# First half's output projection in seven products, with its differences made beside the second input projection; the second half's takes the convolutions' features first

## The chip, the cores and the metric

The kernel runs on one core of one Trainium2 chip. The metric is the device time of one launch in microseconds (us). A core has a TensorE (PE; its weight loads are PEld), a VectorE (DVE), a ScalarE (ACT), a GpSimd (POOL) and a SyncE (SP), which here does nothing but issue DMAs.

## The reference, cut to what matters

One hybrid decoder block over 2048 positions of width 1024, in float32:

```
h = rmsnorm(x) ; proj = h @ w_in                 # columns q k v g a | c_b c_c c_h
o_gla  = rmsnorm(gated_linear_attention(q, k, v, decay(a))) * silu(g)   # 512 wide, a state runs over the chunks
o_conv = c_b * causal_conv3(c_c * c_h)                                  # 512 wide
x = x + concat([o_gla, o_conv]) @ w_out          # the output projection, 1024 x 1024
h2 = rmsnorm(x) ; x = x + (silu(h2 @ w_gate) * (h2 @ w_up)) @ w_down
out = rmsnorm(x)
```

## The kernel before, in words

Features lie on the partitions. The 2048 positions are four blocks of 512 (b = 0 to 3); blocks 0 and 1 are the first half, 2 and 3 the second. Every float32 operand is split into a high and a low part (`split`, L180 and L193/L194: a ScalarE copy that rounds, then a VectorE subtraction), and each 128x128 by 128x512 product is three matmuls: high by high, high by low, low by high.

The input projection and the feed-forward part run in **units** (`unit`, L464): a 2x2 block of weights (A11, A12, A21, A22) times a 2x2 block of activations (B; its two columns are the two blocks of a half, its two rows the two halves of the feature axis) in seven products instead of eight, by Strassen's method in Winograd's form (`PRODUCTS`). A product is 12 matmuls (L460 to L462), a unit 84. VectorE makes the sums of weights S1 to S4 (L435) and splits them; the activations' differences T1 to T4 are made beforehand. The products' results go through PSUM: c11, c22, c12 are copied out by ScalarE (L500) and completed by VectorE additions (`plus`, L489); with `onto` (as in the down projection) all of it is VectorE additions into tiles that are loaded already. A product that accumulates onto the PSUM tile `oa` or `ob` again must wait until the addition before has read it.

Order of the work: `opening` and `in_proj(0)` (first half, twelve units of 84 less the first two), `in_proj(1)` (twelve units), `out_proj(0)`, `out_proj(1)`, then the feed-forward part. Beside them generators run in the background: `tick`, called after each product or k step, takes a step of `background` at every second call, and at some of the others. The gated attention of a half, `gla_half`, has eight chunks of 128 positions; each has six kinds of small matmul: scores (`sc`), transposes (`kt_ps`, `v_ps`), outputs (`o_ps`), state (`kv`) and a transpose of the result (`ot`). A chunk's inputs are loaded from DRAM scratch with 14 loads of 64 KB (`kq`, `ee`, `vt`, `gt`). `gate(1)` makes the second half's decays (`a_ps`, `z`, scans on VectorE).

`gla_finish` and the end of `in_proj` split the finished features and store both parts in DRAM (`s_gla`, `s_mix`). `out_proj` loads them as pairs (`build_mix`: 16 tiles of 512 KB, names `op<-sgla`, `op<-sm`) and does 8 k steps for each pair of output tiles, without Strassen: 2 x 2 x 8 x 3 = 96 matmuls (L1226, L1227, L1229) for each of four d0, 384 for a half, heads k = 0 to 3 first. VectorE adds the residual (L1251), the result is stored (`s_x1`) and its squares are summed (L1208).

The pool `op` has 28 operand tiles. A unit of `in_proj(1)` uses all 28, so that the next stage's loads wait, tile by tile, for the last unit's products, in the order of `PRODUCTS`. All these DMAs are issued by SP in one order, and each waits for an earlier DMA's semaphore; a load that waits holds up those behind it. The tile framework orders each engine's instructions at build time; on the chip each engine runs its own list in that order.

Of the kernel before, what the change touches and what calls it, by code (L numbers as in the profile page):

```python
# [11 lines left out]
F32 = mybir.dt.float32  # L12
# [8 lines left out]
P = 128  # L21
# [10 lines left out]
LAST_GROUP = GROUPS[-1]  # L32
EARLY = 7
EPS = 1e-6

# [18 lines left out]
def tile_hymba_block(ctx, tc, x, xt, win, wa, wgu, wout, wffn, wdown, wdown_first, small, out):  # L54
# [58 lines left out]
    s_x1 = scratch("sx", KD)  # L113
    s_mix = [[dram.tile([P, 2, PB], F32, name=f"sm{b}_{k}") for k in range(4)] for b in range(NB)]
    s_gla = [dram.tile([P, HEADS, 2, PB], F32, name=f"sgla{b}") for b in range(NB)]
    s_act = [
# [143 lines left out]
    background = []  # L260
    pace, ahead, hurry, steady, hasty = [0], [], [], [], []

# [134 lines left out]
    def weight_quarter(src):  # L397

        n = src.shape[-1]
# [7 lines left out]
        split(src, h[:, 0, :], h[:, 1, :])  # L407
        catch_up()
        return h
# [8 lines left out]
    def unit_weights(src, raw=None, between=()):  # L418
        raw = raw_weights(src) if raw is None else raw
        between = iter(between)  # L420
# [4 lines left out]

        n = src.shape[-1]
        a11, a12, a22, a21 = [raw[:, i, :] for i in range(4)]
        s1 = rawp.tile([P, PB], F32, name="s1", tag="s1", bufs=1)[:, 0:n]
        w = {"A11": weight_quarter(a11)}
# [33 lines left out]

    def unit(src, ops, into=None, onto=None, raw=None, between=(), rest=None):  # L464

# [561 lines left out]
    def in_proj(half, ops, raw=None, between=(), rest=None):  # L1027
# [17 lines left out]
        for i0 in (0, 2):  # L1045
# [134 lines left out]
    def gla_finish(b, t, osb, g):  # L1180
# [12 lines left out]
    def plain_weights(src, n):  # L1193

        raw = rawp.tile([P, 4, PB], F32, name="raw", tag="raw")
        load(raw[:, 0:n, :], src)
        for i in range(n):
# [11 lines left out]

    def build_mix(half):  # L1210
        def pair(b, k):
            return load_pair(s_gla[b][:, k] if k < HEADS else s_mix[b][k - HEADS])

        return [[pair(2 * half + j, k) for j in range(2)] for k in range(KD)]

    def out_proj(half, ops, ahead=None, rest=None):
        ssq = []
        ws = chain.from_iterable(plain_weights(wout[u], 4) for u in range(4))
        for d0 in range(0, KD, 2):
            o = {(e, j): bank() for e in range(2) for j in range(2)}  # L1220
            for k in range(KD):
                for e in range(2):
                    wh, wl = next(ws)
                    for j in range(2):
                        m = ops[k][j]
                        pe.matmul(o[e, j][:], wh, m[:, 0, :], start=k == 0, stop=False)  # L1226
                        pe.matmul(o[e, j][:], wh, m[:, 1, :], start=False, stop=False)  # L1227
                    for j in range(2):
                        pe.matmul(  # L1229
                            o[e, j][:], wl, ops[k][j][:, 0, :], start=False, stop=k == KD - 1  # L1230
                        )
                if k == 3:
# [5 lines left out]
                if half:  # L1238
                    for _ in range(1 if d0 == KD - 2 else 2):
                        next(rest if d0 == KD - 2 else ahead, None)  # L1240
                tick()
# [393 lines left out]
    ssq = out_proj(1, build_mix(1), h2_first(ssq, h2), h2_rest(h2))  # L1635
    ahead.append(h2_ahead(ssq))
# [114 lines left out]
```

## Time and profile before

| | us |
|---|---|
| median of 3 runs (2044.63 to 2045.59) | 2045.29 |
| the profiled execution's own time | 2043.05 |
| its span in the trace | 2041.3 |
| PE busy in the span | 2016.8 |
| PEld busy | 1661.9 |
| DVE busy | 1534.8 |
| ACT busy | 976.4 |

The profiled execution's time is 1.75 us longer than its span. Busy times count an instruction from its start to its modelled end, and pipelined instructions overlap: a matmul of 512 columns shows some 0.39 us, and starts come closer together than that. A row of a window view gives the busy time and number of instructions of each engine in a stretch, the granted TensorE clock, the busy share of the 16 DMA engines, and the GB/s moved. A timeline row gives start, duration, engine, line, output<-inputs, and in brackets idle time ahead of it with its releaser.

### The profile page before, as it was taken

How to read it: one execution, taken by the hardware profiler on the slowest of the kernel's cores; microseconds unless marked ns; L12 is line 12 of the kernel's file. 1: busy time of each engine (PE TensorE's matmuls, PEld its weight loads, DVE VectorE, ACT ScalarE, POOL GpSimd, SP SyncE). 2: the span in 40 equal slices, each digit the busy share in tenths (PEclk: the TensorE clock that was granted, in tenths of full speed). 3: DMA queues.
4: the chain of work that ended last, by engine and by line, in shares of the span. 5: the costliest groups of instructions: out<-in, count | busy, mean ns of one | idle time of the engine just before them, and what ended most of it. 6: DMA issues, size and time to landing. Idle time of an engine off the chain costs nothing.

```text
span 2041.3 us, 26875 instructions
## 1 busy us (share of the span) xinstructions
PE 2016.8 (99%) x9295; PEld 1661.9 (81%) x9295; DVE 1534.8 (75%) x2752; ACT 976.4 (48%) x1936; POOL 11.0 (1%) x17
## 2 busy tenths in 40 slices
PE   9999989999999999999999999999999999999997
PEld 8888878887888888888888888887888888888886
DVE  7888966659744697777777688877777767778886
ACT  6664555756543344444444452334534444454344
POOL 0000000000000000000000000000000000000001
PEclk9999999999999999999999999999999999999999
DMA  7356885524675983546445576576444434486653
GB/s 263 118 202 222 288 302 166 159 81 158 240 250 169 366 303 134 189 152 222 179 146 191 213 281 253 187 280 277 157 168 170 164 141 170 179 331 217 248 217 128
DMA packets 190887, 422.51 MB, mean 207 GB/s; under 512 B 20032, under 2 KB 67360, under 8 KB 181280
## 3 DMA queue, kind: packets, MB, share of 16 engines
q1 hardware_dynamic: 189600, 419.76, 58.1%
q8 instruction: 73, 1.20, 0.2%
q10 hardware_dynamic: 1152, 1.05, 0.2%
q14 instruction: 62, 0.51, 0.1%
HBM read 276.02 MB, written 144.70 MB: 206 GB/s over the span
## 4 chain that ended last, share of the span: by engine, by line
PE 92%; DMA 3%; DVE 3%; ACT 1%; issue 0%; SPq 0%; DVEq 0%; ACTq 0%
PE mm L460 25%; PE mm L462 25%; PE mm L461 25%; PE mm L1226 3%; PE mm L1227 3%; PE mm L1229 3%; PE mm L756 1%; PE a_ps L976 1%; PE mm L757 1%; PE mm L758 1%; PE o_ps L1148 1%; PE o_ps L1150 1%; PE mm L1541 1%; DVE wq L194 0%; PE sc L1124 0%
## 5 line engine op out<-in xcount | busy, mean ns | idle before, releaser
L460 PE MATMUL mm<-op,wq 128*128 128x512 f32 x2443 | 949.3, 392 | 8.7 <-ACT c L500 4.2
L461 PE MATMUL mm<-op,wq 128*128 128x512 f32 x2443 | 949.4, 389 | 0.2 <-DVE op L194 0.2
L462 PE MATMUL mm<-op,wq 128*128 128x512 f32 x2443 | 939.8, 390 | 1.4 <-DVE wq L194 1.2
L193 ACT ACTIVATE wq<-raw 128x512 fp32r<-128x512 f32 (+2 forms) x612 | 357.4, 588 | 602.1 <-PE mm L462 486.7
L460 PEld LDWEIGHTS mm<-op,wq 128*128 128x128 f32 x2443 | 458.5, 188 | 109.6 <-ACT c L500 6.4
L462 PEld LDWEIGHTS mm<-op,wq 128*128 128x128 f32 x2443 | 458.5, 188 | 98.6 <-DVE wq L194 2.7
L461 PEld LDWEIGHTS mm<-op,wq 128*128 128x128 f32 x2443 | 458.7, 188 | 95.2 <-DVE op L194 1.5
L194 DVE TENSOR_TENSOR wq<-raw,wq 128x512 fp32r<-128x512 f32 (+2 forms) x612 | 386.0, 636 | 179.6 <-ACT wq L193 178.2
L489 DVE TENSOR_TENSOR c<-mm,c 128x512 f32<-128x512 f32 x196 | 134.8, 688 | 71.6 <-PE mm L462 64.4
L489 DVE TENSOR_TENSOR y<-mm,y 128x512 f32<-128x512 f32 x185 | 126.7, 688 | 49.7 <-PE mm L462 49.2
L500 ACT ACTIVATE c<-mm 128x512 f32<-128x512 f32 x198 | 115.3, 589 | 20.7 <-PE mm L462 16.7
L435 DVE TENSOR_TENSOR raw<-raw 128x512 f32<-128x512 f32 (+2 forms) x192 | 120.3, 632 | 2.2
L193 ACT ACTIVATE wq<-s 128x512 fp32r<-128x512 f32 (+2 forms) x96 | 56.4, 587 | 103.7 <-PE mm L462 98.0
L1226 PE MATMUL mm<-op,wq 128*128 128x512 f32 x256 | 100.7, 397 | 0.4 <-DMA op<-sgla 0.4
L1227 PE MATMUL mm<-op,wq 128*128 128x512 f32 x256 | 99.9, 390 | 0.0
L435 DVE TENSOR_TENSOR s<-raw 128x512 f32<-128x512 f32 (+2 forms) x96 | 60.8, 633 | 35.6 <-DMA raw<-in_wffn_dram 20.0
L1229 PE MATMUL mm<-op,wq 128*128 128x512 f32 x256 | 82.4, 390 | 0.0
L194 DVE TENSOR_TENSOR op<-op 128x512 fp32r<-128x512 f32 x94 | 62.0, 684 | 3.6 <-ACT op L193 3.5
L194 DVE TENSOR_TENSOR wq<-s,wq 128x512 fp32r<-128x512 f32 (+2 forms) x96 | 60.8, 633 | 3.3 <-ACT wq L193 2.5
L435 DVE TENSOR_TENSOR raw<-s,raw 128x512 f32<-128x512 f32 (+2 forms) x96 | 60.8, 634 | 1.4
L193 ACT ACTIVATE op<-op 128x512 fp32r<-128x512 f32 x94 | 54.6, 620 | 7.2 <-DMA op<-sa_T 3.7
L1226 PEld LDWEIGHTS mm<-op,wq 128*128 128x128 f32 x256 | 48.1, 188 | 11.3 <-issue 1.6
(229 smaller groups left out, 1634.8 us busy)
## 6 DMA issues: line engine op xcount, KB each, us to landing
raw<-in_wffn_dram SPq DMA_DIRECT2D x44, 1024.0 KB, 6.0
sa_B<-so SPq DMA_DIRECT2D x47, 512.0 KB, 3.8
op<-sa_B SPq DMA_DIRECT2D x47, 512.0 KB, 7.1
raw<-in_win_dram SPq DMA_DIRECT2D x22, 1024.0 KB, 5.7
sa_T<-so SPq DMA_DIRECT2D x44, 512.0 KB, 4.4
op<-sa_T SPq DMA_DIRECT2D x44, 512.0 KB, 6.9
raw<-in_wdown_dram SPq DMA_DIRECT2D x24, 768.0 KB, 5.4
sx<-y SPq DMA_DIRECT2D x48, 256.0 KB, 3.7
```

The lines of the kernel that those rows point to most:

```text
L193: last_hi[:] = [act.activation(hi, src, AF.Copy)]
L194: last_lo[:] = [dve.tensor_tensor(lo, src, hi.bitcast(F32), ALU.subtract)]
L435: dve.tensor_tensor(*args)
L460: pe.matmul(o[:], wh, xh, start=first and k == 0, stop=False, skip_group_check=True)
L461: pe.matmul(o[:], wh, xl, start=False, stop=False, skip_group_check=True)
L462: return pe.matmul(o[:], wl, xh, start=False, stop=k == n - 1, skip_group_check=True)
L489: last_plus[:] = [dve.tensor_tensor(t[:], o[:], t[:], ALU.add)]
L500: last_out[:] = [act.activation(t[:], o[:], AF.Copy)]
L756: pe.matmul(acc[:], wq[:, 0, c], p[:, 0, :], start=first, stop=False)
L1226: pe.matmul(o[e, j][:], wh, m[:, 0, :], start=k == 0, stop=False)
L1227: pe.matmul(o[e, j][:], wh, m[:, 1, :], start=False, stop=False)
L1229: pe.matmul(o[e, j][:], wl, ops[k][j][:, 0, :], start=False, stop=k == KD - 1)
```

## The change

The first half's output projection becomes four units of seven products (`out_proj_in_sevens`): B is the first half's features (rows: heads k = 0 to 3 and convolution features k = 4 to 7; columns: blocks 0 and 1), 336 matmuls in place of 384. The rounded pairs of the first half are not stored any more: `in_proj(0)` and `gla_finish` for b < 2 store whole features, without a split. A new generator, `mix_differences`, loads them (16 loads of 256 KB), makes T1 to T4 (16 subtractions, 8 splits of T1 and T2) and stores them (24 stores of 256 KB); `tick` steps it at odd calls, from the end of the first half's attention on (`mixes_begin`, ahead of `gate(1)`). `mix_operands` loads all 28 operand tiles: T1 and T2 as pairs of 512 KB, the 20 others whole (256 KB), to be split on arrival: B11 at once, B21, T3, B22 and T4 at `due`. The residuals are loaded after them, for the next unit midway in a unit. `hastened(gla_half(0), 14)` becomes 22. The second half's `out_proj` stays plain, with `LATE_HEADS`: k = 4 to 7 (convolution) first, then the heads. Its core:

```diff
+LATE_HEADS = 4, 5, 6, 7, 0, 1, 2, 3
...
+        elif mixes:
+            next(mixes[0], None)
         elif hasty and pace[0] % 4 == 3:
...
         c22 = copied("c22", ob, (1, 1))
+        due("B21")
         mul(2, oa)
         c12 = copied("c12", oa, (0, 1))
+        if midway is not None:
+            midway()
...
                 dve.tensor_tensor(y[:], c[:], y[:], ALU.mult)
+                if half == 0:
+                    store(s_mix[j][i0 + r][:], y[:])
+                    continue
...
+        if b < 2:
+            store(s_gla[b][:, :, t * P : (t + 1) * P], osb[:])
+            return
...
+    def mix_differences():
...
+        tiles = fetch()
+        yield
+        for k in range(4):
+            b11, b12, b22, b21 = tiles
+            subtract(b11, b12, b11)
+            subtract(b12, b22, b12)
+            store(s_diff["T3"][k][:], b12[:])
+            yield
+            subtract(b22, b22, b11)
+            halved("T1", k, b11)
+            subtract(b21, b21, b22)
+            store(s_diff["T4"][k][:], b21[:])
+            yield
+            halved("T2", k, b22)
+            tiles = fetch()
+            yield
...
+        for _, n in PRODUCTS:
+            ops[n] = [(load_pair if n in ("T1", "T2") else load_undivided)(p) for p in src[n]]
+            if n == "B11":
+                with behind(last_out):
+                    for o in ops[n]:
+                        split(o[:, 1, :].bitcast(F32), o[:, 0, :], o[:, 1, :])
+            elif n not in ("T1", "T2"):
+                undivided[n] = ops[n]
+        return ops
+
+    def out_proj_in_sevens(ops):
...
+        for d0 in range(0, KD, 2):
+            raw = raw_weights(wout[d0 // 2]).rearrange("p a (b e c) -> p (a b) e c", e=2, c=P)
+            quads = [raw[:, 4 * h : 4 * h + 4, e, :] for e, h in ((0, 0), (0, 1), (1, 1), (1, 0))]
+            more = partial(fetch, d0 + 2) if d0 + 2 < KD else None
+            unit(None, ops, onto=onto[d0], raw=quads, midway=more)
...
+        return {k: [pair(2 + j, k) for j in range(2)] for k in LATE_HEADS}
...
-    background.extend([pause(3), hastened(gla_half(0), 14), gate(1, ops)])
+    background.extend([pause(3), hastened(gla_half(0), 22), mixes_begin(), gate(1, ops)])
     in_proj(1, ops)
     drain_background(lambda: (1, PT - 1) in done)
-    ssq = out_proj(0, build_mix(0))
+    ssq = out_proj_in_sevens(mix_operands())
```

What it moves is decided by the order that comes out on each engine. Three places where the prediction stands on it follow.

SP, around the end of the last unit of `in_proj(1)`, before: the last operand pairs of the first half (`op<-sm`), the next attention chunk's 14 loads (the first is shown), and further on the last convolution stores (`sm2_3` is block 2, feature tile 3) and the first residual `y`.

```order
L148 DMA op_5729<-sm0_3_204 128x1024
L148 DMA op_5731<-sm1_3_208 128x1024
L151 DMA sm2_2_211<-hi_5678 128x512
L148 DMA kq_5653<-sk3_0_125 128x128
...
L151 DMA sm2_3_212<-hi_5696 128x512
L151 DMA sm2_3_212<-c11_5199 128x512
L148 DMA y_5837<-in_xt_dram 128x512
L148 DMA raw_6265<-in_wout_dram 128x2048
```

The same place now: `op_5905`, `op_5907`, `op_5909` are T4's tiles for k = 1 to 3.

```order
L157 DMA gt_5802<-sg3_3_168 128x128
L160 DMA sm3_3_216<-hi_5830 128x512
L160 DMA sm3_3_216<-c22_5171 128x512
L160 DMA sm3_2_215<-hi_5836 128x512
L160 DMA sm3_2_215<-c12_5209 128x512
L160 DMA sm2_3_212<-hi_5842 128x512
L160 DMA sm2_3_212<-c11_5340 128x512
L157 DMA op_5905<-sdT4_1_234 128x512
L157 DMA op_5907<-sdT4_2_235 128x512
L157 DMA op_5909<-sdT4_3_236 128x512
L157 DMA y_5911<-in_xt_dram 128x512
```

The stores and the residual kept their places; three operand loads now stand between them, behind the 14 loads of the chunk.

DVE, first unit of the first half's output projection, now (there is no such unit before): L203 are splits of operands (`op_`) and of attention results (`osb_`), L507 is `plus`, `mm_5949` is the PSUM tile `oa` and `y_5911` the residual of the first output; `ot_6145` is an attention transpose on PE.

```order
L1209 SCALAR_TENSOR_TENSOR osb_6014<-ot_6145,sml_99,gt_5629 128x512
L203 TENSOR_TENSOR op_5905<-op_5905 128x512
L203 TENSOR_TENSOR op_5907<-op_5907 128x512
L507 TENSOR_TENSOR y_5911<-mm_5949,y_5911 128x512
L203 TENSOR_TENSOR osb_5717<-osb_5717,gt_5406 128x512
L203 TENSOR_TENSOR op_5909<-op_5909 128x512
L507 TENSOR_TENSOR y_5913<-mm_5963,y_5913 128x512
```

The first addition out of `oa` stands behind two splits of T4's tiles, and T4 is the last product's operand.

PE, the same unit, now: the end of the fourth product (A12 by B21, PSUM tile `mm_6050`), one chunk's small matmuls, and the start of the third product, which accumulates onto `oa` again.

```order
L480 MATMUL mm_6050<-op_5885,wq_5936 128x512
L1148 MATMUL sc_6063<-kq_5799 128x128
L1148 MATMUL sc_6064<-kq_5799 128x128
...
L1154 MATMUL kt_ps_6071<-ident_87,kq_5799 128x128 x2
L1157 MATMUL v_ps_6074<-ident_87,vt_5801 128x128 x4
L1208 MATMUL ot_6145<-ident_87,osb_6014 128x128 x4
L478 MATMUL mm_5949<-op_5871,wq_5933 128x512
```

Ahead of these rows PE has the products by B11 and T1, the transpose `ot_5817`, and one chunk's `o_ps` and `kv`; before the change PE has plain k steps in this place, which wait for nothing but their operand pairs.

More of the change, by code (lines that the diff above doesn't have):

```diff
@@ L113, in tile_hymba_block @@
     s_x1 = scratch("sx", KD)
-    s_mix = [[dram.tile([P, 2, PB], F32, name=f"sm{b}_{k}") for k in range(4)] for b in range(NB)]
-    s_gla = [dram.tile([P, HEADS, 2, PB], F32, name=f"sgla{b}") for b in range(NB)]
+    parts = [[], [], [2], [2]]
+    s_mix = [
+        [dram.tile([P] + parts[b] + [PB], F32, name=f"sm{b}_{k}") for k in range(4)]
+        for b in range(NB)
+    ]
+    s_gla = [dram.tile([P, HEADS] + parts[b] + [PB], F32, name=f"sgla{b}") for b in range(NB)]
+    s_diff = {
+        n: [dram.tile([P, PB] if n in WHOLE else [P, 2, PB], F32, name=f"sd{n}_{k}") for k in range(4)]
+        for n in ("T1", "T2", "T3", "T4")
+    }
     s_act = [
@@ L462, in product_step, with unit @@
         return pe.matmul(o[:], wl, xh, start=False, stop=k == n - 1, skip_group_check=True)
-    def unit(src, ops, into=None, onto=None, raw=None, between=(), rest=None):
+    def unit(src, ops, into=None, onto=None, raw=None, between=(), rest=None, midway=None):
         w = unit_weights(src, raw, between)
@@ L1196, in plain_weights @@
         load(raw[:, 0:n, :], src)
-        for i in range(n):
+        for i in (n // 2 + i if i < n // 2 else i - n // 2 for i in range(n)):
             h = weight_quarter(raw[:, i, :])
@@ L1208, in sum_squares, with mixed, fetch, halved @@
             dve.tensor_tensor(ssq[:], ssq[:], q[:], ALU.add)
-    def build_mix(half):
+    def mixed(b, k):
+        return s_gla[b][:, k] if k < HEADS else s_mix[b][k - HEADS][:]
+    def mix_differences():
+        order = [kj for k in range(4) for kj in ((k, 0), (k, 1), (k + 4, 1), (k + 4, 0))]
+        def fetch():
+            tiles = []
+            for k, j in [order.pop(0) for _ in order[:4]]:
+                tiles.append(bt("h"))
+                load(tiles[-1][:], mixed(j, k))
+            return tiles
+        def halved(n, k, y):
+            hi = bx[0].tile([P, PB], F32R, name="hi", tag="b")
+            with behind(last_out + last_plus):
+                split(y[:], hi[:], y[:].bitcast(F32R))
+            for e, p in enumerate((hi, y)):
+                store(s_diff[n][k][:, e, :], p[:].bitcast(F32))
+        def subtract(y, a, b):
+            with behind(last_plus):
+                dve.tensor_tensor(y[:], a[:], b[:], ALU.subtract)
+        tiles = fetch()
[14 more added lines that the diff above has]
+            yield
@@ L1237, in out_proj @@
                             load(ys[e, j][:], xt[2 * half + j, :, d0 + e, :])
-                if half:
-                    for _ in range(1 if d0 == KD - 2 else 2):
-                        next(rest if d0 == KD - 2 else ahead, None)
+                for _ in range(1 if d0 == KD - 2 else 2):
+                    next(rest if d0 == KD - 2 else ahead, None)
                 tick()
```

63 lines of the change are left out of this document (48 added, 15 removed).

## The prediction

> **What bounds the kernel now.** I read the page's first and fourth parts, then windows of 100 us, then the waits, then timelines of the two places where the change puts its work.
>
> ```profile
> span 2041.3 us, 26875 instructions
> PE 2016.8 (99%) x9295; PEld 1661.9 (81%) x9295; DVE 1534.8 (75%) x2752; ACT 976.4 (48%) x1936; POOL 11.0 (1%) x17
> PE 92%; DMA 3%; DVE 3%; ACT 1%; issue 0%; SPq 0%; DVEq 0%; ACTq 0%
> ```
>
> TensorE carries 92% of the chain that ended last: a matmul taken away is time won, unless PE then waits for something it did not wait for before. What one matmul is worth must not be taken from its 0.39 us duration, but from a full stretch:
>
> ```profile
> 900.00:1000.00 100.00, 100.00 (x443) 82.81 (x442) 79.07 (x126) 44.59 (x78) 0.00 (x0) 1.00 0.51 182
> ```
>
> 443 matmuls in 100 us, at full granted clock (1.00): 0.2257 us each.
>
> **Term 1, the products.** Four units of 84 = 336 matmuls take the place of 384, all of the same 128x512 form. 48 x 0.2257 = **10.8 us less**. Everything else is a question of what PE waits for.
>
> **Term 2, the start of the first unit.** The trace has a place of the same kind: the change from the first to the second input projection, where all 28 operand tiles are loaded anew.
>
> ```profile
> 266.09 0.50 PE L460 MATMUL mm<-op,wq 128*128 128x512 f32 x1 [0.29 <-DMA op<-siB]
> 273.95 0.49 PE L460 MATMUL mm<-op,wq 128*128 128x512 f32 x1 [2.14 <-ACT op L193]
> 264.00:268.00 4.00, 3.33 (x14) 2.11 (x13) 2.05 (x3) 1.75 (x3) 0.00 (x0) 1.00 1.03 403
> 268.00:272.00 4.00, 3.81 (x17) 2.82 (x15) 0.08 (x1) 0.77 (x2) 0.00 (x0) 1.00 1.04 400
> 272.00:276.00 4.00, 1.82 (x7) 1.28 (x8) 3.28 (x6) 3.56 (x8) 0.00 (x0) 1.00 1.01 401
> ```
>
> In these 12 us the DMA engines are full (shares 1.01 to 1.04), and PE starts 14 + 17 + 7 = 38 matmuls where 53 fit: 15 x 0.2257 = 3.4 us lost. So such a change of operands is not free. The output projection of before starts at 559.21 without a loss, since a plain k step needs two tiles at a time. Now its first unit needs tiles of all seven kinds within one unit. Let T0 be the end of the last input product. PE's work from there to the third product, which must wait for the addition `y_5911`, is worked out from these rows:
>
> ```profile
> 554.67 0.60 PE L1184 MATMUL ot<-ident,osb 128*128 128x128 f32 x4
> 555.02 0.47 PE L1226 MATMUL mm<-op,wq 128*128 128x512 f32 x1
> 559.21 0.39 PE L1226 MATMUL mm<-op,wq 128*128 128x512 f32 x1
> 563.30 0.38 PE L1148 MATMUL o_ps<-vt,scores 128*128 128x128 f32 x2
> 565.76 0.50 PE L1226 MATMUL mm<-op,wq 128*128 128x512 f32 x1
> 575.75 0.71 PE L1124 MATMUL sc<-kq 64*128 64x128 f32 x8
> 577.02 0.47 PE L1227 MATMUL mm<-op,wq 128*128 128x512 f32 x1
> ```
>
> Three products are 36 x 0.2257 = 8.1 us; `ot` is 555.02 - 554.67 = 0.35, twice; `o_ps` with `kv` 565.76 - 563.30 = 2.46; `sc`, `kt_ps` and `v_ps` 577.02 - 575.75 = 1.27. Together T0 + 12.5 us. When is the addition done? By VectorE's order it follows two splits of T4's tiles; by SP's order T4's last three tiles and the residual itself are issued behind an attention chunk's 14 loads and six stores. The same part of SP's list in before, where T0 = 559.21:
>
> ```profile
> 555.11 5.37 SPq L148 DMA_DIRECT2D kq<-sk  x4
> 565.96 1.86 SPq L148 DMA_DIRECT2D gt<-sg  x4
> 568.21 0.32 SPq L151 DMA_DIRECT2D sm<-c  x1
> 574.74 0.67 SPq L148 DMA_DIRECT2D y<-in_xt_dram  x1
> y<-in_xt_dram SPq DMA_DIRECT2D x2, 256.0 KB, 5.5
> DMA to landing us min/median/max: 2.7/3.7/6.9
> ```
>
> - Upper end: the queue is as slow as before. The residual's load was issued at 574.74, T0 + 15.5, and landed 5.5 us later: T0 + 21.0. With the addition (0.6, below) the third product starts at T0 + 21.6: PE loses 9.1 us.
> - Lower end: SP waits for nothing. T4's first tile is free nine matmuls before T0 (-2.0 us); 14 loads, 6 stores and 3 loads at 1.86/4 = 0.46 us are 10.7, a landing 3.7: T0 + 12.4. Then VectorE's list decides: after the last transpose four instructions of 0.60 stand up to and with the addition, 2.4 us.
>
> The bytes agree with a value between. From the first operand load to this residual SP issues 28 tiles of operands (8 x 512 KB + 20 x 256 KB = 9.4 MB) and 4.9 MB of weights, chunk inputs, stores and the residual, 14.3 MB. The first load can start when the first matmuls of the last unit's first product are done: six products (16.3), some 4.1 of small matmuls and 2.0 ahead of T0, T0 - 22.4.
>
> ```profile
> 552.00:560.00 8.00, 8.00 (x39) 6.61 (x38) 6.70 (x11) 4.08 (x8) 0.00 (x0) 1.00 1.03 422
> 560.00:568.00 8.00, 8.00 (x50) 6.73 (x49) 3.63 (x9) 3.90 (x15) 0.00 (x0) 1.00 0.68 234
> 588.00:596.00 8.00, 8.00 (x44) 6.40 (x43) 5.36 (x16) 4.75 (x16) 0.00 (x0) 1.00 0.95 303
> ```
>
> At 422 GB/s 14.3 MB take 33.9 us (T0 + 11.5), at 303 47.2 us (T0 + 24.8). I take **6.5 us more**, nearer to the upper end, since SP's list is that of before with 9.4 MB of operands for 8.4. After it nothing else is late there: the next units' residuals and weights are issued a unit ahead. [...]
>
> **Term 3, VectorE and the differences.** They are made beside the second input projection.
>
> ```profile
> 461.60 0.68 DVE L194 TENSOR_TENSOR wq<-raw,wq 128x512 fp32r<-128x512 f32 x1
> 462.20 0.69 DVE L435 TENSOR_TENSOR raw<-raw 128x512 f32<-128x512 f32 x1
> 440.00:460.00 20.00, 20.00 (x89) 16.33 (x88) 8.87 (x15) 8.80 (x17) 0.00 (x0) 1.00 0.15 54
> 460.00:480.00 20.00, 19.55 (x87) 15.79 (x86) 20.00 (x41) 18.41 (x41) 0.00 (x0) 1.00 0.28 84
> 480.00:500.00 20.00, 19.23 (x97) 15.43 (x96) 19.00 (x38) 9.04 (x21) 0.00 (x0) 1.00 0.69 224
> 500.00:520.00 20.00, 20.00 (x102) 16.00 (x101) 11.03 (x25) 9.46 (x26) 0.00 (x0) 1.00 0.30 95
> ```
>
> Starts are 0.60 us apart, so 16 subtractions and 8 splits are 14.4 us. VectorE has 80 - 58.9 = 21.1 us free in 440 to 520, but only 1.0 in 460 to 500, where the gates' scans stand and PE already loses 0.45 + 0.77. The change brings the gates forward (22 hastened steps), so part of the free 11 us ahead is used. Bounds: nothing, if all fits the free time; 4.8 us, if the eight or so instructions that fall among the scans push everything back by 0.60 each. I take **1.0 us more**, near the lower end, since PE's additions have a product (2.7 us) of slack. In the four units themselves VectorE gets, beside the attention, 28 weight splits, 20 sums, 28 additions, 14 sums of squares and 16 splits: 106 x 0.60 = 64 us in over 90 us of PE time. That hides, beyond term 2.
>
> **Term 4, ScalarE's tables.** The order of now has 20 table loads, before 15: the hastened attention runs through the silu units.
>
> ```profile
> 411.42 1.28 ACT L200 ACT_TABLE_LOAD   x1
> 412.71 0.20 ACT L200 ACTIVATE hy<-hl 128x4 f32<-128x4 f32 x1
> 410.00:415.00 5.00, 5.00 (x26) 4.18 (x25) 2.77 (x9) 4.93 (x8) 0.00 (x0) 1.00 0.00 0
> ```
>
> Five more at 1.29 us are 6.5 us where ScalarE has little free; PE lost nothing there. Between 0 and 6.5 I take **0.5 more**, nearest to what PE lost. [...]
>
> **Term 5, what goes.** The first half's features are stored once: one 256 KB store fewer lies among the operand loads of 264 to 272 (`sm0_2<-hi`), 0.65 us at 400 GB/s off the loss there, **0.7 less**. The second half now starts on convolution features, which are stored long before; the wait for a head's pair goes:
>
> ```profile
> 666.79 0.47 PE L1226 MATMUL mm<-op,wq 128*128 128x512 f32 x1 [0.35 <-DMA op<-sgla]
> ```
>
> **0.4 less.** The splits of the first half's features and the plain projection's loads were off the chain: nothing.
>
> **Sum.** -10.8 + 6.5 + 1.0 + 0.5 - 0.7 - 0.4 = -3.9 us. From the profiled execution's 2043.05 (span 2041.3 and 1.75 around it) that is 2039.2; the median of the runs, 2045.29, lies 2.24 above that execution, so I predict 2041.4 us.
>
> **The rivals.**
> - A, the start is covered: SP's queue runs ahead as in the lower end, the stall is 2.4, terms 3 and 4 are nothing: -10.8 + 2.4 - 1.1 = -9.5, 2035.8. For it: PE lost only 3.4 us at the like place with 11.5 MB (16 pairs, 12 whole tiles). Against: T4's position.
> - B, two engines fill up: terms 3 and 4 are 4.8 and 1.0 instead of 1.0 and 0.5. -10.8 + 6.5 + 5.8 - 1.1 = +0.4, 2045.7. For it: VectorE's 39.0 of 40 us in 460 to 500. Against: free time on both sides.
> - C, slower: the start of the first unit becomes a DMA stall of its own. If the 14.3 MB move at 270 GB/s, between the 234 and the 303 above, they need 53.0 us, the residual is there at T0 + 30.6, the third product starts at T0 + 31.2, PE loses 18.7: -10.8 + 18.7 + 1.5 - 1.1 = +8.3, 2053.6. It turns slower than before once the residual lands after some T0 + 22. Against: shares near 1.0 come with 400 GB/s in the operand loads.
> - The change does what it says: the order shows 48 matmuls fewer on PE, so I give no chance to that it doesn't.
>
> **How the numbers follow.** My forecast (between -7 and -1.5 us) has 0.43, A 0.25, B 0.18, C 0.14. A measurement of this kernel can tell about 0.2%, 4.1 us, from no change. Faster by more: A and half of the forecast, 0.46. Within: the other half and B, 0.40. Slower: C, 0.14. The range goes from A with the shortest stall, 2035, to the nearer part of C, 2049, with some 0.06 left below and 0.09 above; the forecast's own is 2038.3 to 2043.8.
>
> **What would show it.** PE has 48 matmuls fewer. In the first unit of `out_proj_in_sevens` its third product waits for VectorE's addition into `y`, and that for the load of `y` or a split of `op`: 2.4 to 9 us in one gap. The stretch with the differences has VectorE near full and PE losing 2 to 3 us there; the silu units lose under 1. At 264 to 276 PE loses less than 3.4. I would be wrong if the gap in the first unit were missing, or several units had one, or PE waited for T1's or T2's pairs.

## The result, and the profile after

The changed kernel takes 2061.28 us (median of 5 runs, 2060.57 to 2063.14), the kernel before 2045.29 (5 runs, 2042.75 to 2046.78): a ratio of 1.0085, 95% interval 1.0073 to 1.0096. It is 16 us slower. The profiled execution took 2062.3 us, 19.2 us more in its span than that of before.

The page of the changed kernel: span, busy times, the granted clock in 40 slices of 51.5 us, the chain that ended last.

```profile
span 2060.5 us, 26992 instructions
PE 2014.2 (98%) x9247; PEld 1658.9 (81%) x9247; DVE 1576.0 (76%) x2820; ACT 995.9 (48%) x1965; POOL 11.0 (1%) x17
PE   9999999999879999999999999999999999999997
PEclk9999999999989999999999999999999999999999
PE 72%; DMA 4%; DVE 3%; SPq 0%; issue 0%; ACT 0%; DVEq 0%; ACTq 0%
```

The 48 matmuls are gone (9247 for 9295). Yet TensorE is busy only 2.6 us less, and its share of the chain fell from 92 to 72%: it waits. The eleventh and twelfth slice (515 to 618 us) show an 8 and a 7, and the twelfth a lower clock. TensorE's waits between 390 and 650 us, of after, then all of those of before:

```profile
engine line waited for: us in total, times, longest us
PE sc L1148 <- DVE kq L1138: 13.9, 3, 8.2
PE mm L478 <- DVE y L507: 6.1, 1, 6.1
PE ot L1208 <- DVE osb L1201: 4.9, 2, 3.5
PE mm L480 <- DVE wq L203: 1.5, 1, 1.5
PE mm L478 <- ACT ee L1158: 0.8, 1, 0.8
```

```profile
PE mm L460 <- ACT c L500: 1.2, 2, 0.8
```

From here on **loss** means: the distances between the starts of TensorE's instructions in the timeline, less 0.2265 us for each one of 512 columns and 0.112 for each of 128. (Both are rounded means, so a stretch can come out a few tenths off.)

| loss of TensorE, us | 200-390 | 390-430 | 430-550 | 550-650 | 650-780 |
|---|---|---|---|---|---|
| before | 7.1 | -0.1 | 3.1 | -0.3 | 1.7 |
| after | 3.3 | 6.8 | 15.2 | 14.5 | 1.1 |

29.4 us more were lost and 10.8 saved: 18.6 of the 19.2; the rest is scattered before and after. Three places hold it.

**The silu units (398 to 406).** TensorE and ScalarE, after:

```profile
398.11 0.39 PE L480 MATMUL mm<-op,wq 128*128 128x512 f32 x1
402.03 1.09 PE L1208 MATMUL ot<-ident,osb 128*128 128x128 f32 x4 [3.53 <-DVE osb L1201]
403.34 0.63 PE L479 MATMUL mm<-op,wq 128*128 128x512 f32 x1
403.77 0.63 PE L480 MATMUL mm<-op,wq 128*128 128x512 f32 x1
405.69 0.40 PE L479 MATMUL mm<-op,wq 128*128 128x512 f32 x1
405.93 0.40 PE L480 MATMUL mm<-op,wq 128*128 128x512 f32 x1
```

```profile
397.26 1.28 ACT L208 ACT_TABLE_LOAD   x1
398.56 0.20 ACT L208 ACTIVATE hl<-hsq 128x4 f32<-128x4 f32 x1
399.07 1.28 ACT L209 ACT_TABLE_LOAD   x1
400.36 0.21 ACT L209 ACTIVATE hy<-hl 128x4 f32<-128x4 f32 x1
```

Two table loads stand in the chain from a chunk's outputs over the reciprocal root to `osb`, which the transposes `ot` need. At the faster pace `ot` comes one product earlier on TensorE's list (24 matmuls of 512 columns behind the `kv` ahead of it, where before has 36 and 48 in these units), and finds it unfinished. Both are needed: at 336 us of after, where no table is loaded, `ot` stands behind 24 too and waits for nothing. Behind the wait of 3.53 us the matmuls start 0.43 us apart for some 2.5 us (403.34, 403.77), then 0.24 again; the granted clock is 0.57 from 402 to 406 us. So this wait costs over 1 us more than itself. After the waits of 8.2 and 6.1 us it is the same; together 18 distances of 0.43 stand behind these three, 18 x 0.20 = 3.6 us.

**The differences (490 to 533).** The chain of waits, SyncE's queue and VectorE, after:

```profile
509.90 8.08 DMA sdT<-h
518.00 0.32 SPq L157
522.63 1.92 DMA gt<-sg
525.27 0.34 DVE kq L1138
525.66 1.22 PE sc L1148 x8
```

```profile
512.51 0.85 SPq L160 DMA_DIRECT2D sgla<-gt  x1
517.36 0.33 SPq L157 DMA_DIRECT2D h<-sm  x1
518.00 1.74 SPq L157 DMA_DIRECT2D kq<-sk  x4
```

```profile
510.19 0.68 DVE L203 TENSOR_TENSOR wq<-s,wq 128x512 fp32r<-128x512 f32 x1
516.78 0.69 DVE L453 TENSOR_TENSOR s<-raw 128x512 f32<-128x512 f32 x1 [5.90 <-DMA raw<-in_win_dram]
```

A difference's store takes 8.08 us to land. SyncE's list stands still from 513.4 to 517.4 at the last load of features (`h<-sm`), and the chunk's 14 loads come behind it, the first only when that store has landed. The weights (`raw`), issued at 508.68, land at 516.7; VectorE, which could have caught up, has nothing to do for 5.9 us. Then everything that it was to do comes at once, and the scores wait 8.22 us for `kq`.

**The first unit (577 to 604).** TensorE and VectorE, after:

```profile
588.41 0.39 PE L480 MATMUL mm<-op,wq 128*128 128x512 f32 x1
594.00 1.22 PE L1148 MATMUL sc<-kq 64*128 64x128 f32 x8 [5.21 <-DVE kq L1138]
596.49 1.06 PE L1208 MATMUL ot<-ident,osb 128*128 128x128 f32 x4
603.61 0.80 PE L478 MATMUL mm<-op,wq 128*128 128x512 f32 x1 [6.06 <-DVE y L507]
```

```profile
600.80 1.30 DVE L203 TENSOR_TENSOR op<-op 128x512 fp32r<-128x512 f32 x2 [2.46 <-ACT op L202]
602.86 0.69 DVE L507 TENSOR_TENSOR y<-mm,y 128x512 f32<-128x512 f32 x1 [0.76 <-DMA y<-in_xt_dram]
```

```profile
575.00:590.00 15.00, 13.80 (x75) 10.98 (x73) 15.00 (x28) 11.92 (x29) 0.00 (x0) 1.00 0.87 312
```

T0 is 577.2; the third product starts at 603.61, T0 + 26.4, where 12.5 us of work stand before it. The residual landed at T0 + 25.7 behind two splits of T4, as the order had it; but the chunk's scores wait in the same unit, and VectorE (in the window row, the third number with a count) is busy 15.0 of 15 us.

### The profile page after: what moved, and what is told of

It reads as the page before. It is cut to its first block, busy times and chain, and to the rows that moved or that the text cites. A ratio compares the mean times of both kernels' runs of the same rounds, so it can differ in the third digit from the quotient of the medians.

```text
span 2060.5 us, 26992 instructions
## 1 busy us (share of the span) xinstructions
PE 2014.2 (98%) x9247; PEld 1658.9 (81%) x9247; DVE 1576.0 (76%) x2820; ACT 995.9 (48%) x1965; POOL 11.0 (1%) x17
## 4 chain that ended last, share of the span: by engine, by line
PE 72%; DMA 4%; DVE 3%; SPq 0%; issue 0%; ACT 0%; DVEq 0%; ACTq 0%
PE mm L480 22%; PE mm L478 22%; PE mm L479 22%; PE mm L1343 1%; PE mm L1341 1%; PE mm L1340 1%; DMA op<-sdT 1%; PE mm L1654 1%; DMA raw<-in_wffn_dram 1%; DVE wq L203 0%; SPq L157 0%; DMA op<-shT 0%; DMA sdT<-h 0%; DMA sx<-y 0%; PE a_ps L997 0%
## 5 line engine op out<-in xcount | busy, mean ns | idle before, releaser
L478 PE MATMUL mm<-op,wq 128*128 128x512 f32 x2555 | 997.1, 393 | 12.0 <-DVE y L507 7.1
L479 PE MATMUL mm<-op,wq 128*128 128x512 f32 x2555 | 995.0, 390 | 0.5 <-DVE op L203 0.5
L480 PE MATMUL mm<-op,wq 128*128 128x512 f32 x2555 | 985.1, 390 | 2.2 <-DVE wq L203 1.8
L202 ACT ACTIVATE wq<-raw 128x512 fp32r<-128x512 f32 (+2 forms) x620 | 362.4, 588 | 595.0 <-PE mm L480 508.6
L478 PEld LDWEIGHTS mm<-op,wq 128*128 128x128 f32 x2555 | 480.8, 188 | 117.9 <-DVE y L507 7.9
L480 PEld LDWEIGHTS mm<-op,wq 128*128 128x128 f32 x2555 | 480.7, 188 | 105.1 <-DVE wq L203 4.4
L479 PEld LDWEIGHTS mm<-op,wq 128*128 128x128 f32 x2555 | 481.0, 188 | 100.5 <-DVE op L203 2.8
L203 DVE TENSOR_TENSOR wq<-raw,wq 128x512 fp32r<-128x512 f32 (+2 forms) x620 | 392.9, 638 | 148.5 <-ACT wq L202 146.9
L507 DVE TENSOR_TENSOR y<-mm,y 128x512 f32<-128x512 f32 x213 | 146.2, 689 | 66.0 <-PE mm L480 64.8
L507 DVE TENSOR_TENSOR c<-mm,c 128x512 f32<-128x512 f32 x196 | 135.1, 689 | 62.7 <-PE mm L480 59.9
L453 DVE TENSOR_TENSOR raw<-raw 128x512 f32<-128x512 f32 (+2 forms) x200 | 126.2, 637 | 2.3
L453 DVE TENSOR_TENSOR s<-raw 128x512 f32<-128x512 f32 (+2 forms) x100 | 63.7, 637 | 51.5 <-DMA raw<-in_wffn_dram 28.1
L203 DVE TENSOR_TENSOR op<-op 128x512 fp32r<-128x512 f32 x114 | 75.8, 688 | 7.2 <-ACT op L202 6.8
L202 ACT ACTIVATE op<-op 128x512 fp32r<-128x512 f32 x114 | 66.5, 620 | 12.4 <-DMA op<-sa_T 4.6
L203 DVE TENSOR_TENSOR wq<-s,wq 128x512 fp32r<-128x512 f32 (+2 forms) x100 | 63.7, 637 | 1.8 <-ACT wq L202 1.0
L573 ACT ACTIVATE sg<-mm 128x512 f32<-128x512 f32 x26 | 15.5, 598 | 83.2 <-PE mm L480 83.2
L573 ACT ACTIVATE c<-c 128x512 f32<-128x512 f32 x78 | 49.0, 629 | 11.6 <-DVE c L507 8.6
L1340 PE MATMUL mm<-op,wq 128*128 128x512 f32 x128 | 50.2, 392 | 0.0
L1341 PE MATMUL mm<-op,wq 128*128 128x512 f32 x128 | 49.8, 389 | 0.0
```

What stands on the lines that cost most here:

```text
L202: last_hi[:] = [act.activation(hi, src, AF.Copy)]
L203: last_lo[:] = [dve.tensor_tensor(lo, src, hi.bitcast(F32), ALU.subtract)]
L453: dve.tensor_tensor(*args)
L478: pe.matmul(o[:], wh, xh, start=first and k == 0, stop=False, skip_group_check=True)
L479: pe.matmul(o[:], wh, xl, start=False, stop=False, skip_group_check=True)
L480: return pe.matmul(o[:], wl, xh, start=False, stop=k == n - 1, skip_group_check=True)
```

## The experiments

All are edits of the changed kernel, except where it is said. The losses of their profiled executions by stretch, beside the median and the ratio to the kernel before with its interval (the kernel before was run anew beside each group, at 2043.4 to 2045.3 us, so runs are best compared by the ratio):

| | us | ratio, interval | 390-430 | 430-550 | 550-650 |
|---|---|---|---|---|---|
| after | 2061.28 | 1.0085 (1.0073, 1.0096) | 6.8 | 15.2 | 14.5 |
| e1 | 2058.07 | 1.0072 (1.0057, 1.0087) | 7.1 | 12.1 | 13.3 |
| e2 | 2066.60 | 1.0113 (1.0097, 1.0128) | 6.7 | 15.5 | 17.4 |
| e3 | 2062.04 | 1.0086 (1.0070, 1.0103) | 0.1 | 16.5 | 20.3 |
| e4 | 2044.27 | 1.0001 (0.9991, 1.0010) | 0.1 | 3.0 | 0.7 |
| e5 | 2051.32 | 1.0032 (1.0019, 1.0045) | 7.1 | 2.6 | 16.7 |
| e6 | 2048.28 | 1.0017 (1.0007, 1.0026) | 8.0 | 2.0 | 12.0 |
| e7 | 2049.14 | 1.0025 (1.0015, 1.0034) | 6.9 | 4.5 | 11.2 |
| e8 | 2058.78 | 1.0068 (1.0053, 1.0083) | 7.2 | 4.1 | 21.6 |
| e9 | 2058.36 | 1.0070 (1.0055, 1.0085) | 7.2 | 10.4 | 11.4 |
| e10 | 2060.42 | 1.0077 (1.0060, 1.0094) | 7.1 | 14.0 | 10.9 |
| e11 | 2061.33 | 1.0083 (1.0068, 1.0098) | 0.0 | 14.3 | 14.5 |
| e12 | 2061.34 | 1.0081 (1.0064, 1.0099) | 7.0 | 15.2 | 11.9 |
| e13 | 2062.96 | 1.0089 (1.0074, 1.0104) | 5.5 | 15.9 | 14.6 |
| e14 | 2052.53 | 1.0041 (1.0026, 1.0056) | 8.0 | 14.2 | 5.0 |
| e15 | 2066.43 | 1.0108 (1.0093, 1.0123) | 6.7 | 15.9 | 17.4 |
| e16 | 2066.64 | 1.0110 (1.0093, 1.0127) | 6.4 | 20.9 | 8.2 |
| e17 | 2050.04 | 1.0027 (1.0016, 1.0039) | 6.5 | 6.1 | 12.5 |
| e18 | 2051.02 | 1.0040 (1.0027, 1.0052) | 0.0 | 9.3 | 14.8 |

**e4, the second half alone** (on the kernel before: the new order of k and of the weights).

```diff
-        return [[pair(2 * half + j, k) for j in range(2)] for k in range(KD)]
+        return {k: [pair(2 * half + j, k) for j in range(2)] for k in (LATE_HEADS if half else range(KD))}
```

> The kernel before with only the second half's new order of k (convolution features first). Theory: it takes the wait for a head's pair away and nothing else: PE's loss at 650 to 680 falls from 1.8 to under 0.5 us, the time is 2043.5 to 2045. Rival: the order of k is itself part of the slowdown, since the weights are split in another order: over 2047.

2044.27, no difference. The slowdown is the first half's alone.

**e3, the pace.**

```diff
-hastened(gla_half(0), 22)
+hastened(gla_half(0), 14)
```

> Only the 22 hastened steps go back to 14. Theory T: the loss of 6.8 us at 390 to 425, where the attention's table loads now stand among the silu units and the transposes wait for VectorE (3.5 and 1.4 us), goes to nothing, as before the change. The differences then start later: if there is room, the time is some 2054; if they then meet the gates and the convolutions more tightly, part of it comes back at 480 to 560 and the time is 2055 to 2060. Rival: the loss there has nothing to do with the pace; the time stays within 2059 to 2063.

The loss at 390 to 430 goes as expected, so the table loads and the pace made it: with 14 steps there are 15 table loads again, and `ot` stands behind 36 and 48 matmuls. The time stays: the differences start later, and 1.3 + 5.8 us more are lost further on. Taking a loss away in one stage did not bring time, since the next stage got its work later.

**e5, e6, e7, the differences taken apart.** e5 leaves the generator out; e6 leaves out `subtract` and `split`; e7 leaves out `load` and `store`:

```diff
-background.extend([pause(3), hastened(gla_half(0), 22), mixes_begin(), gate(1, ops)])
+background.extend([pause(3), hastened(gla_half(0), 22), gate(1, ops)])      # e5
-                dve.tensor_tensor(y[:], a[:], b[:], ALU.subtract)                # e6
-                load(tiles[-1][:], mixed(j, k))                                  # e7
-            store(s_diff["T3"][k][:], b12[:])                                    # e7, and the like
```

> The differences T1 to T4 are left out (no loads, no arithmetic, no stores; the products read whole features in their place, so the output is not the block's). All else of the change stays. If the differences make the whole loss at 480 to 560, that stretch falls from 14.4 us to the 1.9 of before, and the time from 2061 to some 2048.5; the loss at 390 to 425 (6.8) and that at 576 to 615 (14.8) stay, since neither has a difference in it. Rival: the loss at 480 to 560 is the attention's, which runs elsewhere now; then over 6 us of it stay and the time is over 2052.

> The differences' 16 loads and 24 stores stay, with their buffers and their places on SP; the 16 subtractions and 8 splits are left out (the stored tiles are the unchanged features, so the output is not the block's). Theory P (transfers and buffers: SP's list, the 11 buffers that they share with the attention's chunk, 10.5 MB more): over half of the 12.4 us that the differences cost at 480 to 560 stays, time 2055 or more. Theory V (VectorE and ScalarE: 14.4 us more work where VectorE had 1.0 free of 40): under a third stays, time under 2053.

> The 16 subtractions and 8 splits stay, on a constant and without any transfer; their 16 loads and 24 stores are left out, and the products read whole features (the output is not the block's). Theory P: under a third of the 12.4 us stays, time under 2053. Theory V: over half stays, time 2055 or more. If the two parts cost about 6 each, or neither costs much alone, it is their chain (a store that waits for VectorE, a chunk's load that waits for the store).

Without the differences 2.6 us are lost at 430 to 550 (before: 3.1), so they make the whole loss there, 12.6 us. Either part alone costs almost nothing: 2.0 us are lost with the transfers, 4.5 with the arithmetic (e7's trace is of its fastest execution, 2.3 us under its median). So it is the two together that cost. How they do is read from the trace above: they are tied to each other, a store waits for VectorE, the next load for the store's landing and for its buffer, the attention's loads and the weights for SyncE's list, and VectorE for the weights. A rival is not excluded by these three runs: that both use up the same spare time, and only their sum exceeds it.

**e1, the differences' transfers on GpSimd's queue.**

```diff
-                load(tiles[-1][:], mixed(j, k))
+                pool.dma_start(tiles[-1][:], mixed(j, k))
-            store(s_diff["T3"][k][:], b12[:])
+            pool.dma_start(s_diff["T3"][k][:], b12[:])
```

> Only the 16 loads and 24 stores of the differences move from SP to GpSimd's own queue; the work on VectorE and ScalarE stays. Theory Q (one queue in order): PE's loss of 12.7 us at 480 to 528 (2.0 before the change) comes from SP's list, in which a difference's load or store waits at the head for VectorE and holds up the weights and the attention chunk behind it; it should fall to 2 to 4 us, and the time from 2061 to some 2051. Rival V (VectorE is full): 16 subtractions and 8 splits push everything back there, whoever issues the transfers; the loss stays over 10 us and the time within 2058 to 2062.

At 430 to 550 12.1 us are lost for 15.2, not 2 to 4; the times can hardly be told apart. Being in one list with the differences is not all of it. In e1 one of SyncE's loads waits 3.3 us for TensorE's `kv`, which releases a chunk's buffer (the differences' tiles share these 11), `ee` lands late again, and ScalarE waits for it. A wait of SyncE, a row of ScalarE and the first of TensorE's waits, all of e1:

```profile
SPq L157 <- PE kv L1179: 3.3, 1, 3.3
```

```profile
494.97 0.42 ACT L1135 ACTIVATE ee<-ee 128x256 f32<-128x256 f32 x1 [2.95 <-DMA ee<-sd]
```

```profile
PE mm L478 <- ACT c L518: 7.2, 3, 5.3
```

Behind `ee` on ScalarE stands the copy of a product's result, and behind that TensorE, 5.3 us.

**e8, T1 and T2 whole.**

```diff
-                split(y[:], hi[:], y[:].bitcast(F32R))
-            for e, p in enumerate((hi, y)):
-                store(s_diff[n][k][:, e, :], p[:].bitcast(F32))
+            store(s_diff[n][k][:], y[:])
-            if n == "B11":
+            if n in ("B11", "T1", "T2"):
```

> T1 and T2 are stored and loaded whole (256 KB) and split on arrival, as the other kinds: 8 splits, 8 buffers and 8 stores fewer beside the second input projection, 2.1 MB fewer among the 14.3 MB at the first unit, and 8 splits of 0.60 us more there, ahead of the second and third product. Theory B (bytes bound the first unit, 2.1 MB at 380 GB/s are 5.5 us): the loss at 576 to 615 falls from 14.8 to 9 or 10, and that at 480 to 560 by 3 to 6, time some 2052. Rival V at that place: the 4.8 us of splits more hold VectorE, which is full at 580 to 596, and the loss at 576 to 615 stays or grows to 19, time 2057 to 2063.

At 430 to 550 the loss falls to 4.1, with 8 splits, 8 buffers and 8 stores fewer, as the tie and its rival would both have it. But the first unit loses 21.6, 19.0 of them in one wait of the attention's transposes for `osb`, which VectorE had behind the splits that were moved there. The rival at that place held.

**e2 and e9, other queues for the operands and for the chunk.**

```diff
+        queues.append(nc.gpsimd)                                   # e2, around the 28 operand loads
-                load(dst[:, i, :], r[:, s])
+                (nc.sync if b < 2 else pool).dma_start(dst[:, i, :], r[:, s])   # e9
```

> Only the 28 operand loads of the first half's output projection move from SP to GpSimd's queue. Theory Q: PE's loss of 14.8 us at 576 to 615 comes from SP's list, where the attention chunk's 14 loads and the residual stand behind operand loads that wait for their tiles; the wait of the scores (5.2 us) goes, the wait for the residual's addition (6.1 us) falls to under 3, and the time falls by 7 to 10 us to some 2053. Rival B (bytes): 14.3 MB have to come in whoever issues them; the loss stays at 12 to 15 us and the time within 2058 to 2062.

> Only the second half's attention chunks' loads (14 of 64 KB each) move from SP to GpSimd's queue. Theory Q (what costs is that a chunk's loads stand in SP's list behind stores of differences, at 480 to 560, and behind operand loads, at 576 to 615): the scores' waits for the scaled kq (13.9 us in all) fall to under 4 us, the time falls by 7 to 11 us to some 2052. Rival (the chunk is only the last of several late things: bytes and VectorE's own list hold the rest): the waits change their names, the time stays over 2057.

With the operands on their own queue the wait for `y` falls to 0.3 us, as expected, but 7.2 us are lost for `osb` instead: VectorE waits 5.8 us for weights that come in beside the operands (its row in e2 below). With the chunk's loads moved, the scores' waits for `kq` are gone, and the wait for `y` grows from 6.1 to 8.0. Moving one transfer ahead put another one last: 11 to 17 us stay.

```profile
580.05 0.69 DVE L455 TENSOR_TENSOR s<-raw 128x512 f32<-128x512 f32 x1 [5.76 <-DMA raw<-in_wout_dram]
```

**e10 and e11, the residual asked for first, and with 14.**

```diff
         onto = {}
         fetch(0)
+        ops = mix_operands()
```

> As the run before, and the first unit's residuals are asked for ahead of the operand loads; VectorE's first addition then stands ahead of the splits of T4. Theory Q: the third product's wait (6.1 us) falls to under 3 as well, and the time to some 2048. Rival B (the 14.3 MB bound the first unit): the loss at 560 to 615 stays over 11 us and the time is within 1 us of the run before.

> As the run before, with 14 hastened steps for 22. The loss of 6.8 us at 390 to 425 goes. With the chunk's loads off SP the later start of the differences costs less than the 6.8 us that it gave back when 14 was tried alone: some 2043 to 2046, as the kernel before or a little under it. Rival: gates, convolutions and differences still meet on VectorE, the gain is given back, within 2 us of the run before.

Nothing gained, but the order that was to be tried did not come out. In the list that SyncE ran in e10 the residual's load still stands behind all 28 operand loads (issued at 586.89, the last operands' from 584.18 to 585.86), and VectorE's first addition behind all 16 operand splits, both as in e9; in e11 it is the same. So these two runs say nothing on a residual that comes first. In e10 VectorE was busy up to the moment at which the residual landed; both were late alike:

```profile
593.29 0.69 DVE L203 TENSOR_TENSOR op<-op 128x512 fp32r<-128x512 f32 x1
594.38 0.69 DVE L507 TENSOR_TENSOR y<-mm,y 128x512 f32<-128x512 f32 x1 [0.40 <-DMA y<-in_xt_dram]
```

**e12, fewer bytes.**

```diff
+            if n == "T2":
+                ops[n] = ops["T1"]
+                continue
```

> T2's four pairs are not loaded, the products read T1's tiles in their place (the output is not the block's): 2.1 MB of 14.3 fewer at the first unit, no instruction of VectorE or ScalarE more or less. Theory B: the loss at 560 to 615 falls by 2.1 MB at some 390 GB/s, 5.4 us, from 14.7 to some 9, time 2056. Theory Q and V (order and VectorE): it falls by under 2 us, time over 2059.

2.6 us less are lost at 550 to 650, half of what the bytes would give; the time does not move. Bytes are a part at most.

**e14, the first unit copied by ScalarE.**

```diff
-            unit(None, ops, onto=onto[d0], raw=quads, midway=more)
+            if d0 == 0:
+                c = {at: bt("c") for at in onto[d0]}
+                unit(None, ops, into=c, raw=quads, midway=more)
+                for at, y in onto[d0].items():
+                    dve.tensor_tensor(y[:], c[at][:], y[:], ALU.add)
```

> Only the first of the four units is changed: its products are copied out of PSUM by ScalarE into fresh tiles and the residuals added afterwards, as many VectorE instructions as before, 4 ScalarE copies more. Theory L (VectorE's list and the residual's load hold the first addition): the wait for the addition into y (6.1 us) goes and nothing as large takes its place; the loss at 576 to 615 falls from 14.8 to 6 to 9, of which the wait for the chunk's kq (5.2) stays; time 2053 to 2056. Rival B (the operands are not there yet): the third product waits for T2's tiles or the fourth for B21's, and the loss stays over 12 us.

This run takes most of the loss at the third place away. Same bytes, same queue, same number of VectorE instructions: the loss falls from 14.5 to 5.0, the time by 8.8 us. The windows of after (above) and of e14:

```profile
575.00:590.00 15.00, 13.94 (x76) 11.09 (x74) 12.72 (x27) 9.38 (x26) 0.00 (x0) 1.00 0.91 334
590.00:605.00 15.00, 14.12 (x63) 11.24 (x64) 14.63 (x26) 12.18 (x25) 0.00 (x0) 0.89 0.98 336
```

TensorE is busy 14.1 us from 590 to 605, where after has 4.9. The wait of 6.1 us was for the instruction that frees the PSUM tile `oa`: with `onto` it is an addition that needs the residual and VectorE's turn, with a copy it needs neither. The wait for the chunk's `kq` (5.2 us), which was to stay, went too, and not through the copy: the lists came out in another order. In e14 the scores stand 48 matmuls of 512 columns behind the `kv` ahead of them, in after 12, and VectorE begins the 16 operand splits at 590.64, in after at 580.23. So the order on the engines, and not the bytes, made most of the loss there; how much of the 8.8 us is the copy's and how much the other order's, this run doesn't tell.

**e13 and e15, arithmetic on GpSimd.**

```diff
+    def split_aside(src, hi, lo):
+        act.activation(hi, src, AF.Copy)
+        return pool.tensor_tensor(lo, src, hi.bitcast(F32), ALU.subtract)
-                dve.tensor_tensor(y[:], a[:], b[:], ALU.subtract)
+                pool.tensor_tensor(y[:], a[:], b[:], ALU.subtract)   # e13; e15: split_aside in `due`
```

> The differences' 16 subtractions and the subtracting half of the 8 splits run on GpSimd (1.30 us each for 128x512 by the page's last part of the kernel, 31 us in all, where it had nothing to do); transfers, buffers and SP's list stay. Theory V with the chain: VectorE is relieved of 24 x 0.60 = 14.4 us, the loss at 425 to 560 (14.9) falls to 3 to 6, time 2050 to 2053. Rival: GpSimd's slower tiles hold their buffers and the queue longer, the attention chunk's loads come later still; the loss stays over 10 us, time over 2057.

> Only the subtracting half of the 16 operand splits in the first unit (B21, T3, B22, T4) runs on GpSimd, 1.30 us each, in place of 0.60 on VectorE. Theory L: VectorE has 9.6 us less to do between 577 and 603, the kq scaling and the first addition come earlier; the loss at 576 to 615 falls to 8 or 10 us, or, if GpSimd's 20.8 us for the 16 become what the fourth product waits for, a new wait of PE for GpSimd's op tiles of 3 to 6 us shows. Rival B: nothing falls, 14 us or more.

No gain in e13, 5 us lost in e15, and neither theory had the reason. A row of each engine in e13, and one of each in e15, at the same time:

```profile
481.26 6.95 POOL L1263 TENSOR_TENSOR h<-h 128x512 f32<-128x512 f32 x4
485.30 1.77 DVE L1091 TENSOR_TENSOR c<-c,c 128x512 f32<-128x512 f32 x1
```

```profile
578.95 3.26 POOL L208 TENSOR_TENSOR op<-op 128x512 fp32r<-128x512 f32 x2 [577.14 <-ACT op L207]
579.28 1.78 DVE L203 TENSOR_TENSOR wq<-raw,wq 128x512 fp32r<-128x512 f32 x1
```

While GpSimd computed, these two instructions of VectorE took 1.77 and 1.78 us, where the same forms take 0.69 in the mean in after (0.71 at most), and GpSimd's own took 1.44 and 1.63 us in the mean in e13, where it takes 1.29 for 128x512 in after. What VectorE was relieved of it lost again: over the whole span it is busy 1576.0 us in after, 1576.8 in e13 with 24 instructions fewer, and 1576.3 in e15 with 16 fewer.

**e16, e17, e18, joined.** e16 is e14 with e9 and e13; e17 is e14 with e8; e18 is e17 with 14 hastened steps.

> e14, the second half's chunk loads on GpSimd's queue (e9) and the differences' subtractions on GpSimd (e13) together. If the three losses are separate: 6.8 at 390 to 425 stays, 480 to 560 falls to 3, 560 to 615 to 3 to 5; time 2043 to 2046, level with the kernel before. Rival: GpSimd's arithmetic holds up the chunk's loads in its one list, and the attention waits again: time over 2050.

> e14 and e8 together: the first unit copied by ScalarE, T1 and T2 whole and split on arrival. If the losses add up: 390 to 425 keeps its 7 to 8 us, 425 to 560 has the 4.2 of e8 in place of e14's 14.3, and the first unit, with 8 splits of 0.60 us more ahead of the second and third product, 4.1 to 9: from e14's 2052.5 to 2043 to 2047. Rival: the 8 splits bring the first unit's wait back whole (e8 had 21.4 us from 560 to 615): over 2055.

> e17 with 14 hastened steps for 22. If the losses add up, the 7 to 8 us at 390 to 425 go, and the differences, which start later, give back 2 to 4 of them: 3 to 6 us under e17, some 2040 to 2042, a little under the kernel before. Rival: as in e3, the differences then run into the convolutions and the first unit, and all of it is given back: within 2 us of e17.

e16 went the rival's way, over 2050: 20.9 us are lost at 430 to 550. e17 is the fastest of all that keep the change and compute the block, 2050.04, still 0.27% slower than the kernel before (0.16 to 0.39%). It lies between its two cases: 6.1 us at 430 to 550, but 9.4 us in one wait for `osb` ahead of the first unit. In e18 that wait stays, the 6.5 us at 390 to 430 go, and 3.2 + 2.3 come back in the next two stretches. The largest waits between 425 and 650, of e17 and of e18:

```profile
PE ot L1208 <- DVE osb L1201: 9.4, 1, 9.4
```

```profile
PE ot L1208 <- DVE osb L1201: 10.0, 1, 10.0
```

The losses do not add up, and no version beats the kernel before.

## Why the prediction was wrong

- **Term 1 held**: 48 matmuls fewer, 10.8 us.
- **Term 5 was small by its size**: -0.7 and -0.4 were given; the loss fell by 3.8 at 200 to 390 (1.9 of it at 264 to 276) and by 0.6 at 650 to 780. In e4, with the second half's order alone, it fell by the same 0.6.
- **Term 2 failed, and it is the largest miss: +6.5 (2.4 to 9.1) against +14.8.** The addition, its place behind T4's splits and the residual's late load were all seen. Two steps failed. First, "After it nothing else is late there": the chunk's 14 loads, which the text itself placed ahead of the residual in SyncE's list, were late themselves, and the scores lost 5.2 us before the addition lost 6.1. Second, "106 x 0.60 = 64 us in over 90 us of PE time. That hides": it was a mean over four units, and a large part of it falls before the first addition; from 575 to 590 VectorE is busy 15.0 of 15. The time that TensorE lost behind such waits in after, 0.20 us for each of 5 to 7 slow matmuls, was in no term. e14, with copies and another order of the lists, loses 9.5 us less there.
- **Term 3 failed: +1.0 (0 to 4.8) against +12.1.** Only the 24 instructions on VectorE were priced. The 40 transfers of the differences were listed with the change and stood in no term, although each waits in SyncE's one list and holds one of 11 buffers. e6 and e7 show that the arithmetic alone, which was priced, costs 1.4 us over before. The two together cost the rest.
- **Term 4 failed, just past its upper bound: +0.5 (0 to 6.5) against +6.9.** "PE lost nothing there" was read at the old pace, where the transposes came a product later. e3 shows the loss goes with the pace.
- **The rivals.** C, the slower one (0.14), came nearest: it had the residual later than T0 + 22, 18.7 us lost, 2053.6. The residual came at T0 + 25.7. But bytes were its reason, and e12 and e14 show them to be a part at most. B gave the second place 4.8 us of its 12.1 and laid it to VectorE's work, which alone costs 1.4 (e7).
- **The signs named in advance**: one gap in the first unit was forecast, there were two; the stretch with the differences was to lose 2 to 3 us and lost 15.2; the silu units were to lose under 1 and lost 6.8. All three say where it was wrong. At 264 to 276 less than 3.4 was to be lost, and 2.3 were.

What stays open: how the 8 us of the store at 509.90 divide between its wait among other transfers and its own time (the DMA engines are busy 0.99 of it, at 303 GB/s); whether the differences cost by the tie or by the sum of their work; how e14's gain divides between the copy and the order; and whether more buffers or a residual that comes first would help, which no run tries.

## What to carry to other kernels

A transfer that waits for arithmetic and an arithmetic instruction that waits for a transfer, in lists that run in order, must be priced together: here each alone cost 0 to 1.4 us and both 12. A share of busy time over a stage does not hide work that is due at its start; count what stands in the list ahead of the instruction that frees the next tile, and let that instruction need as little as possible (a copy for an addition, with the other order of the lists that came with it, was worth 8.8 us). Where a wait is taken away, look what stands next in its engine's list: in most of these runs it was another wait. And where an edit is to change an order, read from the lists whether it did: in e10 it did not, and in e14 more moved than was meant.

## What the runs showed of the hardware

- Behind TensorE idle times of 3.53, 8.22 and 6.06 us in after 5 to 7 matmuls start 0.43 us apart, at a granted clock of 0.57 (402 to 406), 0.54 (528 to 532) and 0.53 (603.6 to 607); behind 1.36 us (at 419.18) none do. Behind 5.21 us, where small matmuls come next, the clock is 0.50 (594 to 597). The length of the wait alone does not decide it here: 8 such distances follow an idle time of only 1.79 us in e2 and 7 follow 1.72 in e14, but none follow 1.72 in e17, nor 3.52 in e13 (at 400.16, clock 1.00). What decides it is not shown.
- Two instructions of VectorE that ran while GpSimd computed took 1.77 us (`c<-c,c` in e13, at 485.30) and 1.78 us (`wq<-raw,wq` in e15, at 579.28); in after the same forms take 0.69 in the mean and 0.71 at most. Why they took longer is not shown.
- A store of 256 KB took 8.08 us to land at 509.90, where 2.6 is the median of the 16 stores of its kind. From 509.9 to 518 the DMA engines were busy 0.99 of the time.

```profile
sdT<-h SPq DMA_DIRECT2D x16, 256.0 KB, 2.6
```
